# Gate and up of the second feed-forward as seven quarter products (one level of Strassen's algorithm)

## The chip, the cores and the metric

The kernel runs on one core of one Trainium2 chip. The metric is the time of one execution on the device in microseconds (us); lower is better. A core has five engines that run their own instruction queues in order and meet through semaphores: TensorE (PE in the profile; its weight loads have a row of their own, PEld), VectorE (DVE), ScalarE (ACT), GpSimd (POOL) and SyncE (SP), which here issues all DMAs.

## What is computed

Two layers of a transformer over 512 latent and 256 context tokens, model width 1024. Each layer has a token mixer (windowed attention in the first, chunked retention in the second) and a feed-forward, each behind a modulated RMS norm and with a gated residual. After the second layer only the latent tokens are wanted. What the change touches is that layer's feed-forward:

```
def modulate(h, shift, scale):
    return h * (1 + scale) + shift

def swiglu(h, w_in, w_out):
    gate, up = jnp.split(h @ w_in, 2, axis=-1)
    return (jax.nn.silu(gate) * up) @ w_out

x = x + mx[5] * swiglu(modulate(rms_norm(x, norm2_g[i]), mx[3], mx[4]), ffn_w_in[i], ffn_w_out[i])
```

Its hidden width is 2816, which is 22 column tiles of 128. Everything is float32.

## The kernel before, in words

Activations lie transposed: a tile is 128 features (partitions) by tokens, so the 1024 features of the latent stream are eight tiles of 128x512.

**Three matmuls for one.** A float32 product is made of three fast ones. Each operand is split into a rounded part (hi, `fp32r`) and the rest (lo = value - hi). `mm3` (L134) issues hi*hi, lo*hi and hi*lo into the same PSUM tile; `project` (L142) does so for the eight feature tiles, 24 matmuls in a row. Weights go through `next_w` (L120): a DMA brings 128x1024 floats into `wraw` (two buffers), ACT casts them to `whi` (L130), DVE subtracts to get `wlo` (L131). A pair whi/wlo lives in a buffer of the pool `rp` or of the stage's own pool, two of each, in turn. `split` (L146) does the same for activations: ACT casts (L147), DVE subtracts (L148).

**The last head of the retention mixer** ends with `out_tile` (L1019): for each half of the tokens (`HALVES`, 256 each) and each of eight output tiles d, twelve matmuls into a PSUM tile `pv`, then DVE's gated add into the residual `res` (L1027), then ACT's square and DVE's running sum (`add_square`, L191 and L192). After a half is done, `rms` makes the reciprocal root on PE (L199), ACT (L102, L178) and DVE (L179, L180), and `modulate` (L208) makes that half of the feed-forward's operand: DVE multiplies into `hn` (L211), ACT adds the shift and rounds to hi (L214), DVE makes lo (L215). The first half's modulation stands in the middle of the second half's output tiles.

**The feed-forward**, `ffn` (L757), runs over the column tiles in groups of 2, 4, 4, 4, 4 and 4 (`FFN_GROUPS`). `hidden` (L765) makes one tile: `project` with the gate's weights and with the up's weights into the two halves of the PSUM tile `gu` (twice 24 matmuls of 512 columns; the first two tiles go by halves of 256 tokens, so that they can begin when half of the operand is there), then SiLU on ACT (L107), the product with up on DVE (L785), and a split into `ax`. `output` (L791) multiplies a finished group with its rows of the output weights: eight output tiles d, for a group of four 12 matmuls of 512 columns each into `pj` (two PSUM buffers), and DVE's gated add (L225). It stands behind the first hidden tile of the next group. The last one writes the result out by DMA.

**Order.** The code above gives instructions in program order; a scheduler then sets each engine's static order from its own estimate of readiness, and buffers are handed out in that order. On the chip each engine runs its queue strictly as set.

Of the kernel before, what the change touches and what calls it, by code (L numbers as in the profile page):

```python
# [9 lines left out]
F32R = mybir.dt.float32r  # L10
# [4 lines left out]
P = 128  # L15
D = 1024
KT = D // P
SX = 512
SC = 256
# [11 lines left out]
HALVES = (slice(0, 256), slice(256, 512))  # L31
# [21 lines left out]
def dit_kernel(ctx, tc, xT, cT, crow, small, consts, masks, tabs0, tabs1, jtab, adaQ, adaN, adaT, wst, out):  # L53
    nc = tc.nc
    mult, add, sub = ALU.mult, ALU.add, ALU.subtract
# [21 lines left out]
    mods = {(l, s): cp.tile([P, 6, 8], F32, name=f"mod{l}{s}") for l in range(2) for s in range(2)}  # L77
# [28 lines left out]
    def silu(out_, in_):  # L106
        ins = nc.scalar.activation(out_, in_, AF.Silu)  # L107
        after(ins, turn["silu"][:1] or turn["lnexp"])
        turn["silu"].append(ins)
# [7 lines left out]

    wpos, wsel = [0], [0]

    def next_w(pool, own=2):  # L120

        raw = T(rp, 1024, "wraw", 2)
        nc.sync.dma_start(raw, wst[wpos[0]])
        bufs = own
        if wsel[0] % (2 + own) < 2:
            pool, bufs = rp, 2
        wpos[0] += 1
        wsel[0] += 1
        hi, lo = T(pool, 1024, "whi", bufs, F32R), T(pool, 1024, "wlo", bufs, F32R)
        nc.scalar.copy(hi, raw)  # L130
        nc.vector.tensor_tensor(lo, raw, hi, op=sub)  # L131
        return hi, lo
# [9 lines left out]
    def project(w, hs, o):  # L142
        for k in range(KT):
            mm3(o, (w[0][:, k * P:(k + 1) * P], w[1][:, k * P:(k + 1) * P]), hs[k], k == 0, k == KT - 1)

    def split(t, hi, lo):  # L146
        nc.scalar.copy(hi, t)  # L147
        return nc.vector.tensor_tensor(lo, t, hi, op=sub)  # L148


    def load_stream(s):
        res = []
        if s == 0:
            for k in range(KT):
                t = T(rp, 512, "res", 12)
                nc.sync.dma_start(t, xT[:, k, :])
                res.append(t)
        else:
            for k in range(0, KT, 2):
                t = T(rp, 512, "res", 12)  # L160
# [41 lines left out]
    def h_tiles(s):  # L202
        hi = T(rp, 512, "h", 24, F32R)
        if s == 0:
            return hi, T(rp, 512, "h", 24, F32R)
        return hi[:, 0:SC], hi[:, SC:2 * SC]

    def modulate(l, s, which, k, res, h, c=slice(None), tmp=t_hn):  # L208
        y = ssq[s][:, c]
        t = tmp(y.shape[1])  # L210
        nc.vector.scalar_tensor_tensor(t, res[k][:, c], acol[l, s, which][:, k:k + 1], y, mult, mult)  # L211
        hi, lo = h[0][:, c], h[1][:, c]
        b = mods[l, s][:, 3 * which, k:k + 1]
        nc.scalar.activation(hi, t, AF.Identity, bias=b)  # L214
        return nc.vector.scalar_tensor_tensor(lo, t, b, hi, add, sub)  # L215
# [8 lines left out]
    def gated_add(s, l, part, d, o, res):  # L224
        nc.vector.scalar_tensor_tensor(res[d], o, mods[l, s][:, part, d:d + 1], res[d], mult, add)  # L225
# [105 lines left out]
    h = [[], []]  # L331
    raw = []
# [360 lines left out]
    t1 = cp.tile([P, 8], F32, name="lg_t1")  # L693
    t2 = cp.tile([P, 8], F32, name="lg_t2")
# [33 lines left out]
    xr = load_stream(0)  # L728
# [25 lines left out]
    A.close()  # L754


    def ffn(l, streams, hs, halves, extra, done, ahead=()):  # L757


        F = ExitStack()  # L760
        psF = F.enter_context(tc.tile_pool(name="psF", bufs=1, reuse_waits="tile", space=PSUM))
        fp = F.enter_context(tc.tile_pool(name="fp", bufs=1, reuse_waits="tile"))
        count = [0]

        def hidden(act, first):  # L765
            w = ahead.pop(0) if ahead else [next_w(fp), next_w(fp)]
            if count[0] == SHIFT_AT:
                wsel[0] += 2
            for s, _ in streams:
                n = NTOK[s]  # L770
                if s == 0:
                    gu = T(psF, 1024, "gu", 2)
                    hi, lo = T(fp, 512, "ax", 11, F32R), T(fp, 512, "ax", 11, F32R)
                else:
                    gu = T(psF, 512, "guc", 2)
                    hl = T(fp, 512, "ac", 6, F32R)
                    hi, lo = hl[:, 0:SC], hl[:, SC:]
                go, uo = gu[:, 0:n], gu[:, n:2 * n]
# [6 lines left out]
                nc.vector.tensor_tensor(t, t, uo, op=mult)  # L785
                last = split(t, hi, lo)
                act[s].append((hi, lo))
            extra(count[0], first, fp, [last])
            count[0] += 1

        def output(act, gsz, final):  # L791
            nd = 1024 // (gsz * P)
            w = []

            def one(s, res, d):
                while len(w) * nd <= d:
                    w.append(next_w(fp))
                wd = w[d // nd]
                o = pj(NTOK[s])
                for k in range(gsz):  # L800
                    c0 = k * nd * P + (d % nd) * P
                    mm3(o, (wd[0][:, c0:c0 + P], wd[1][:, c0:c0 + P]), act[s][k], k == 0, k == gsz - 1)
                gated_add(s, l, 5, d, o, res)
                if final:
                    done(s, d, res[d])

            if final:
                for s, res in streams:
                    for d in range(KT):
                        one(s, res, d)  # L810
            else:
                for d in range(KT):
                    for s, res in streams:
                        one(s, res, d)

        prev = None
        for gsz in FFN_GROUPS:
            act = {s: [] for s, _ in streams}
            for f in range(gsz):
                hidden(act, f == 0)  # L820
                if f == 0 and prev is not None:
                    output(*prev, False)
            prev = (act, gsz)
        output(*prev, True)
        F.close()
# [27 lines left out]
    hx, _ = norm_mod(0, 0, 1, xr)  # L853
    hc, _ = norm_mod(0, 1, 1, cres)
# [12 lines left out]
    h = [norm_mod(1, 0, 0, xr)[0], norm_mod(1, 1, 0, cres)[0]]  # L867
# [36 lines left out]
    for hd in range(RH):  # L904

        o = []
        for i in range(2):
            w = wq[i] if hd == 0 else next_w(qp)
# [5 lines left out]
        o = []  # L914
# [68 lines left out]
        r, z = mv[:, 8:12], mv[:, 12:16]  # L983
# [19 lines left out]
        for e in range(4):  # L1003
            w = next_w(qp)
            go = pj()
# [23 lines left out]
        if hd < RH - 1:  # L1029
            for d in range(KT):  # L1030
                out_tile(d, slice(0, SX))
            continue
        hx = [h_tiles(0) for _ in range(KT)]
        ln_exp_turn()
        for i, c in enumerate(HALVES):
            for d in range(KT):
                out_tile(d, c)
                add_square(0, d, xr[d], c)
                if i == 1 and d == 1:
                    rms(0, HALVES[0])  # L1040
                    for k in range(KT):
                        modulate(1, 0, 1, k, xr, hx[k], HALVES[0])
        ahead = [[next_w(None), next_w(None)]]
        rms(0, HALVES[1])
        for k in range(KT):
            modulate(1, 0, 1, k, xr, hx[k], HALVES[1])
    R.close()

    ffn(1, ((0, xr),), (hx,), 2, lambda *_: None, lambda s, k, t: nc.sync.dma_start(out[:, k, :], t), ahead)

# [141 lines left out]
```

## Time and profile before

| | |
|---|---|
| median of 3 runs | 1854.78 us (1852.64 to 1856.34) |
| the profiled execution | 1854.34 us |
| its span, first to last instruction | 1852.5 us (1.8 us lie around it) |
| mean granted TensorE clock | 0.993 |
| first and last matmul of the second feed-forward | start at 1485.65 and 1848.41 us of the span |
| first matmul of its third column tile | 1510.78 us |

Times on a row of the trace are microseconds from the start of the span, then the duration of the row. "x2" means two instructions shown as one row. In square brackets stands how long the engine sat idle before, and the engine, tile and line that ended the wait. In the groups by line, the numbers after the bar are the busy time in us and the mean duration of one instruction in ns. A matmul's duration reaches from its issue to its last result, so that neighbours overlap; the time that it takes from the engine is the distance from one start to the next, called the pitch below. The same holds in a small way for DVE and ACT.

### The profile page before, as it was taken

How to read it: one execution, taken by the hardware profiler on the slowest of the kernel's cores; microseconds unless marked ns; L12 is line 12 of the kernel's file. 1: busy time of each engine (PE TensorE's matmuls, PEld its weight loads, DVE VectorE, ACT ScalarE, POOL GpSimd, SP SyncE). 2: the span in 40 equal slices, each digit the busy share in tenths (PEclk: the TensorE clock that was granted, in tenths of full speed). 3: DMA queues.
4: the chain of work that ended last, by engine and by line, in shares of the span. 5: the costliest groups of instructions: out<-in, count | busy, mean ns of one | idle time of the engine just before them, and what ended most of it. 6: DMA issues, size and time to landing. Idle time of an engine off the chain costs nothing.

```text
span 1852.5 us, 24666 instructions
## 1 busy us (share of the span) xinstructions
PE 1798.5 (97%) x9969; PEld 1517.3 (82%) x9969; DVE 1032.3 (56%) x1808; ACT 629.2 (34%) x1064; POOL 150.1 (8%) x243
## 2 busy tenths in 40 slices
PE   5999999899999999999999999999999999999999
PEld 4877776788888888888878888888888888888887
DVE  6787776978555545363684552653543663443343
ACT  5576676351211212121252322422322442222221
POOL 0044443310000000000010010010010000000000
PEclk9999999999999999999999999999999999999999
DMA  9100035525323324261521220320321133333332
GB/s 344 47 24 24 1 108 159 190 93 158 114 92 105 102 91 151 85 205 52 167 82 35 80 80 23 98 85 21 94 69 46 57 99 96 102 92 102 92 102 80
DMA packets 50946, 177.98 MB, mean 96 GB/s; under 512 B 5648, under 2 KB 6032, under 8 KB 50576
## 3 DMA queue, kind: packets, MB, share of 16 engines
q1 hardware_dynamic: 50832, 176.41, 29.9%
q8 instruction: 78, 1.28, 0.3%
q14 instruction: 36, 0.29, 0.1%
HBM read 174.29 MB, written 2.10 MB: 95 GB/s over the span
## 4 chain that ended last, share of the span: by engine, by line
PE 86%; DVE 6%; ACT 3%; DMA 2%; POOL 2%; issue 2%; SPq 0%; DVEq 0%; ACTq 0%; POOLq 0%
PE pj L138 9%; PE pj L139 9%; PE pj L140 9%; PE gu L138 9%; PE gu L139 9%; PE gu L140 9%; PE guc L140 2%; PE guc L139 2%; PE guc L138 2%; PE pT L635 2%; PE pv L138 2%; PE pv L140 2%; PE pv L139 2%; PE pv L943 2%; PE pv L944 2%; PE pv L942 2%
## 5 line engine op out<-in xcount | busy, mean ns | idle before, releaser
L130 ACT CAST whi<-wraw 128x1024 fp32r<-128x1024 f32 x212 | 222.2, 1048 | 387.8 <-PE pj L140 200.5
L131 DVE TENSOR_TENSOR wlo<-wraw,whi 128x1024 fp32r<-128x1024 f32 x212 | 264.7, 1248 | 153.3 <-ACT whi L130 152.5
L138 PE MATMUL gu<-h,whi 128*128 128x512 f32 (+1 forms) x736 | 281.0, 383 | 3.0 <-DVE res L1027 3.0
L139 PE MATMUL gu<-h,wlo 128*128 128x512 f32 (+1 forms) x736 | 280.8, 383 | 0.0
L140 PE MATMUL gu<-h,whi 128*128 128x512 f32 (+1 forms) x736 | 280.4, 382 | 0.0
L138 PE MATMUL pj<-h,whi 128*128 128x512 f32 (+1 forms) x512 | 185.3, 362 | 6.9 <-DVE res L225 6.1
L139 PE MATMUL pj<-h,wlo 128*128 128x512 f32 (+1 forms) x512 | 182.1, 356 | 1.0 <-DVE wlo L131 1.0
L140 PE MATMUL pj<-h,whi 128*128 128x512 f32 (+1 forms) x512 | 181.9, 356 | 0.0
L225 DVE SCALAR_TENSOR_TENSOR res<-pj,mod,res 128x512 f32<-128x512 f32 (+1 forms) x160 | 104.7, 656 | 128.7 <-PE pj L140 128.6
L138 PEld LDWEIGHTS gu<-h,whi 128*128 128x128 f32 x736 | 139.4, 190 | 28.7 <-ACT h L214 3.2
L140 PEld LDWEIGHTS gu<-h,whi 128*128 128x128 f32 x736 | 139.6, 190 | 26.3
L139 PEld LDWEIGHTS gu<-h,wlo 128*128 128x128 f32 x736 | 139.4, 190 | 25.4
L248 DVE CUSTOM_DVE_ANT_0 junk<-adaw,crow_sb,small_sb 128x1024 bf16<-128x1024 f32 x100 | 134.9, 1349 | 36.7 <-DMA adaw<-in_adaT_dram 32.9
L138 PE MATMUL pj<-ax,whi 128*128 128x512 f32 x352 | 138.4, 393 | 0.0
L139 PE MATMUL pj<-ax,wlo 128*128 128x512 f32 x352 | 137.5, 391 | 0.0
L140 PE MATMUL pj<-ax,whi 128*128 128x512 f32 x352 | 137.0, 390 | 0.0
L107 ACT ACTIVATE hn<-gu 128x512 f32<-128x512 f32 x44 | 26.3, 598 | 285.3 <-PE gu L140 285.3
L138 PEld LDWEIGHTS pj<-h,whi 128*128 128x128 f32 x512 | 98.7, 193 | 21.0 <-DVE res L225 7.2
L139 PEld LDWEIGHTS pj<-h,wlo 128*128 128x128 f32 x512 | 98.6, 193 | 13.0 <-DVE wlo L131 1.4
L140 PEld LDWEIGHTS pj<-h,whi 128*128 128x128 f32 x512 | 98.6, 193 | 12.1 <-issue 0.4
L785 DVE TENSOR_TENSOR hn<-hn,gu 128x512 f32<-128x512 f32 x44 | 30.2, 687 | 134.6 <-ACT hn L107 134.6
L140 PE MATMUL guc<-h,whi 128*128 128x256 f32 x352 | 99.8, 284 | 0.0
(249 smaller groups left out, 3417.6 us busy)
## 6 DMA issues: line engine op xcount, KB each, us to landing
wraw<-in_wst_dram SPq DMA_DIRECT2D x214, 512.0 KB, 3.5
adaw<-in_adaT_dram SPq DMA_DIRECT2D x68, 512.0 KB, 4.0
adan<-in_adaQ_dram SPq DMA_DIRECT2D x16, 512.0 KB, 8.1
wraw<-in_adaN_dram SPq DMA_DIRECT2D x12, 512.0 KB, 4.0
res<-in_xT_dram SPq DMA_DIRECT2D x16, 256.0 KB, 4.8
res<-in_cT_dram SPq DMA_DIRECT2D x8, 256.0 KB, 6.8
crow_sb<-in_crow_dram SPq DMA_DIRECT2D x2, 1024.0 KB, 6.0
out_dram<-res SPq DMA_DIRECT2D x8, 256.0 KB, 2.0
```

The costliest lines, as they stand in the source:

```text
L130: nc.scalar.copy(hi, raw)
L131: nc.vector.tensor_tensor(lo, raw, hi, op=sub)
L138: nc.tensor.matmul(o, whi, xhi, start=first, stop=False)
L139: nc.tensor.matmul(o, wlo, xhi, start=False, stop=False)
L140: nc.tensor.matmul(o, whi, xlo, start=False, stop=last)
L225: nc.vector.scalar_tensor_tensor(res[d], o, mods[l, s][:, part, d:d + 1], res[d], mult, add)
L248: after(nc.vector.tensor_tensor_reduce(junk, w, row, 1.0, bias, mult, add, col), behind)
L635: nc.tensor.transpose(tp[:, a * P:(a + 1) * P], self.pr[(0, 2, 1, 3)[a]][:, ki * P:(ki + 1) * P], ident)
L785: nc.vector.tensor_tensor(t, t, uo, op=mult)
L942: nc.tensor.matmul(vo, hi[:, tok], wk_[0][:, cs], start=k == 0, stop=False)
L943: nc.tensor.matmul(vo, hi[:, tok], wk_[1][:, cs], start=False, stop=False)
L944: nc.tensor.matmul(vo, lo[:, tok], wk_[0][:, cs], start=False, stop=k == KT - 1)
```

## The change

The operand A (tokens by features) is cut in two along tokens and in two along features: A11 is tokens 0 to 255 with features 0 to 511, A12 has the other features, A21 and A22 the other tokens. The weights B of one column tile are cut along features and into gate and up: B11 and B21 are the gate's feature halves, B12 and B22 the up's. From the third column tile on, gate and up (four blocks of 256 tokens by 128 columns) come from seven products of quarters instead of eight:

```
S1 = A21+A22  S2 = S1-A11  S3 = A11-A21  S4 = A12-S2
T1 = B12-B11  T3 = B22-B12  T2 = B22-T1  -T4 = B21-T2
P1 = A11*B11  P2 = A12*B21  P3 = S4*B22  P4' = A22*(-T4)  P5 = S1*T1  P6 = S2*T2  P7 = S3*T3
gate, tokens 0-255   = P1+P2              up, tokens 0-255   = P1+P6 + P5+P3
gate, tokens 256-511 = P1+P6+P7+P4'       up, tokens 256-511 = P1+P6+P7 + P5
```

- `modulate` gets an optional target: for this norm the product before the shift is kept in eight more tiles `hm` (tag `h`) instead of the two rotating `hn` buffers.
- `sums`, called ahead of the second column tile, makes S1 to S4 from `hm` and the shifts in place, 16 DVE instructions of 256 columns, and splits them into 16 tiles `sA`: eight casts on ACT and eight subtractions on DVE, 512 columns each.
- `hidden_seven` makes a column tile from the third on. Per tile: two DMAs as before; three pairs whi/wlo and one half pair (B22, in two tiles of tag `h`) instead of two pairs; four DVE subtractions of 512 columns for the T's; seven products of four feature tiles by three matmuls of 256 columns (84 matmuls instead of 48 of 512 columns) in the PSUM tiles X, Y, Z; four ACT copies out of PSUM; three DVE additions of 256 columns; SiLU in two halves; the product with up and its split as before. Y is accumulated on after each copy: P1, then P6, then P7, then P4'; so the product that follows a copy by one has to wait until the copy has read.
- The pool of the second feed-forward has four pairs whi/wlo of its own instead of two, and two raw buffers of its own.
- The first feed-forward, the first two column tiles of the second and the outputs keep their arithmetic.

```diff
-    def next_w(pool, own=2):
-        raw = T(rp, 1024, "wraw", 2)
+    def w_raw(pool=None, bufs=2):
+        raw = T(pool or rp, 1024, "wraw", bufs)
         nc.sync.dma_start(raw, wst[wpos[0]])
...
-    def modulate(l, s, which, k, res, h, c=slice(None), tmp=t_hn):
+    def modulate(l, s, which, k, res, h, c=slice(None), t=None):
         y = ssq[s][:, c]
-        t = tmp(y.shape[1])
+        if t is None:
+            t = t_hn(y.shape[1])
...
+        own = 4 if hm else 2
+        def sums():
+            q1, q2 = HALVES
+            shift = mods[l, 0][:, 3]
+            sh2 = T(fp, 8, "sh2", 1)
+            nc.vector.tensor_tensor(sh2[:, 0:4], shift[:, 0:4], shift[:, 4:8], op=add)
+            for k in range(4):
+                t1, t2 = hm[k], hm[k + 4]
+                nc.vector.scalar_tensor_tensor(t2[:, q2], t1[:, q2], sh2[:, k:k + 1], t2[:, q2], add, add)
+                nc.vector.tensor_tensor(t1[:, q2], t1[:, q1], t1[:, q2], op=sub)
+                nc.vector.scalar_tensor_tensor(t1[:, q1], t2[:, q2], shift[:, k:k + 1], t1[:, q1], sub, sub)
+                nc.vector.scalar_tensor_tensor(t2[:, q1], t2[:, q1], shift[:, k + 4:k + 5], t1[:, q1], add, sub)
+                for t in (t2, t1):
+                    sA.append((T(fp, 512, "sA", 16, F32R), T(fp, 512, "sA", 16, F32R)))
+                    split(t, *sA[-1])
+        def hidden_seven(act):
+            g, u = w_raw(fp, 2), w_raw()
...
+            split(g, *b["11"])
+            nc.vector.tensor_tensor(g[:, l_], u[:, l_], g[:, l_], op=sub)
+            split(u[:, r_], *b["22"])
+            nc.vector.tensor_tensor(u[:, l_], u[:, r_], u[:, l_], op=sub)
+            nc.vector.tensor_tensor(u[:, r_], u[:, r_], g[:, l_], op=sub)
+            nc.vector.tensor_tensor(g[:, r_], g[:, r_], u[:, r_], op=sub)
+            split(u, *b["32"])
+            split(g, *b["14"])
...
+            product(Y, "11", "11", 0, True)
+            nc.scalar.copy(p1, Y)
+            product(Z, 1, "14", 0, True)
+            nc.scalar.copy(z1, Z)
+            product(Y, 2, "32", 512, False)
+            nc.scalar.copy(u2, Y)
+            product(X, "12", "11", 512, True)
+            nc.vector.tensor_tensor(t[:, HALVES[0]], p1, X, op=add)
+            silu(t[:, HALVES[0]], t[:, HALVES[0]])
+            product(Y, 3, "32", 0, False)
+            nc.scalar.copy(u3, Y)
+            product(Z, 4, "22", 0, False)
+            nc.vector.tensor_tensor(up[:, HALVES[0]], u2, Z, op=add)
+            product(Y, "22", "14", 512, False)
+            nc.vector.tensor_tensor(up[:, HALVES[1]], u3, z1, op=add)
+            silu(t[:, HALVES[1]], Y)
+            nc.vector.tensor_tensor(t, t, up, op=mult)
...
         def hidden(act, first):
-            w = ahead.pop(0) if ahead else [next_w(fp), next_w(fp)]
+            if hm and count[0] >= 2:
+                return hidden_seven(act)
+            if hm and count[0] == 1:
+                sums()
+            w = ahead.pop(0) if ahead else [next_w(fp, own), next_w(fp, own)]
...
+        hm = [T(rp, 512, "h", 24) for _ in range(KT)]
```

More of the change, by code (lines that the diff above doesn't have):

```diff
@@ L118, in dit_kernel, with w_parts @@
     wpos, wsel = [0], [0]
-    def next_w(pool, own=2):
-        raw = T(rp, 1024, "wraw", 2)
+    def w_raw(pool=None, bufs=2):
+        raw = T(pool or rp, 1024, "wraw", bufs)
         nc.sync.dma_start(raw, wst[wpos[0]])
+        wpos[0] += 1
+        return raw
+    def w_parts(pool, own=2):
         bufs = own
@@ L126, in next_w @@
             pool, bufs = rp, 2
-        wpos[0] += 1
         wsel[0] += 1
-        hi, lo = T(pool, 1024, "whi", bufs, F32R), T(pool, 1024, "wlo", bufs, F32R)
+        return T(pool, 1024, "whi", bufs, F32R), T(pool, 1024, "wlo", bufs, F32R)
+    def next_w(pool, own=2):
+        raw = w_raw()
+        hi, lo = w_parts(pool, own)
         nc.scalar.copy(hi, raw)
@@ L754, in dit_kernel, with ffn @@
     A.close()
-    def ffn(l, streams, hs, halves, extra, done, ahead=()):
+    def ffn(l, streams, hs, halves, extra, done, ahead=(), hm=None):
         F = ExitStack()
@@ L763, in ffn @@
         count = [0]
-        def hidden(act, first):
-            w = ahead.pop(0) if ahead else [next_w(fp), next_w(fp)]
+        own = 4 if hm else 2
+        sA = []
+        def sums():
[12 more added lines that the diff above has]
+                    split(t, *sA[-1])
@@ new lines, in operand_a, with product @@
+        def operand_a(n):
+            if isinstance(n, int):
+                return lambda k: [a[:, HALVES[n % 2 if n < 3 else n == 3]] for a in sA[2 * k + (n in (2, 3))]]
+            c, k0 = HALVES[n[0] == "2"], 4 * (n[1] == "2")
+            return lambda k: [a[:, c] for a in hs[0][k0 + k]]
+        def hidden_seven(act):
+            g, u = w_raw(fp, 2), w_raw()
+            b = {"11": w_parts(fp, own)}
+            b["22"] = T(rp, 512, "h", 24, F32R), T(rp, 512, "h", 24, F32R)
+            b["14"], b["32"] = w_parts(fp, own), w_parts(fp, own)
+            l_, r_ = slice(0, 512), slice(512, 1024)
+            split(g, *b["11"])
[6 more added lines that the diff above has]
+            split(g, *b["14"])
+            def product(o, a, n, c0, first):
+                x = operand_a(a)
+                for k in range(4):
+                    ws = slice(c0 + k * P, c0 + (k + 1) * P)
+                    (whi, wlo), (xhi, xlo) = (a[:, ws] for a in b[n]), x(k)
+                    for i, (p, r) in enumerate(((whi, xhi), (wlo, xhi), (whi, xlo))):
+                        nc.tensor.matmul(o, p, r, start=first and k + i == 0, stop=k == 3 and i == 2,
+                                         skip_group_check=not first)
+            X, Y, Z = (T(psF, 512, n, 2)[:, 0:SC] for n in "XYZ")
+            t, up = t_hn(SX), t_sq(SX)
+            e1, e2 = T(rp, 512, "res", 12), T(rp, 512, "res", 12)
+            p1, z1, u2, u3 = e1[:, HALVES[0]], e1[:, HALVES[1]], e2[:, HALVES[0]], e2[:, HALVES[1]]
+            product(Y, "11", "11", 0, True)
[15 more added lines that the diff above has]
+            nc.vector.tensor_tensor(t, t, up, op=mult)
+            hi, lo = T(fp, 512, "ax", 11, F32R), T(fp, 512, "ax", 11, F32R)
+            split(t, hi, lo)
+            act[0].append((hi, lo))
+            count[0] += 1
@@ L771, in hidden @@
                 if s == 0:
-                    gu = T(psF, 1024, "gu", 2)
+                    gu = None if hm else T(psF, 1024, "gu", 2)
                     hi, lo = T(fp, 512, "ax", 11, F32R), T(fp, 512, "ax", 11, F32R)
@@ L777, in hidden @@
                     hi, lo = hl[:, 0:SC], hl[:, SC:]
-                go, uo = gu[:, 0:n], gu[:, n:2 * n]
+                go, uo = (gu[:, 0:n], gu[:, n:2 * n]) if gu else (T(psF, 512, "X", 2), T(psF, 512, "Y", 2))
                 for c in HALVES if count[0] < halves else (slice(0, n),):
@@ L796, in one @@
                 while len(w) * nd <= d:
-                    w.append(next_w(fp))
+                    w.append(next_w(fp, own))
                 wd = w[d // nd]
@@ L1041, in dit_kernel @@
                     for k in range(KT):
-                        modulate(1, 0, 1, k, xr, hx[k], HALVES[0])
+                        modulate(1, 0, 1, k, xr, hx[k], HALVES[0], hm[k][:, HALVES[0]])
         ahead = [[next_w(None), next_w(None)]]
@@ L1045, in dit_kernel @@
         for k in range(KT):
-            modulate(1, 0, 1, k, xr, hx[k], HALVES[1])
+            modulate(1, 0, 1, k, xr, hx[k], HALVES[1], hm[k][:, HALVES[1]])
     R.close()
-    ffn(1, ((0, xr),), (hx,), 2, lambda *_: None, lambda s, k, t: nc.sync.dma_start(out[:, k, :], t), ahead)
+    ffn(1, ((0, xr),), (hx,), 2, lambda *_: None, lambda s, k, t: nc.sync.dma_start(out[:, k, :], t), ahead, hm)
 def _cols(w, n0, n):
```

## Prediction

> **What bounds the kernel now.** The first view is the page's summary: busy time of each engine and the shares of the chain that ended last.
>
> ```profile
> span 1852.5 us, 24666 instructions
> ...
> PE 1798.5 (97%) x9969; PEld 1517.3 (82%) x9969; DVE 1032.3 (56%) x1808; ACT 629.2 (34%) x1064; POOL 150.1 (8%) x243
> ...
> PE 86%; DVE 6%; ACT 3%; DMA 2%; POOL 2%; issue 2%; SPq 0%; DVEq 0%; ACTq 0%; POOLq 0%
> ```
>
> TensorE is the bound: busy for 97% of the span and 86% of the chain. Whether this holds where the change acts, the windows say: the third to the last column tile with all outputs, and one whole group (four hidden tiles and an output).
>
> ```profile
> core 0: us, PE busy (x) PEld busy (x) DVE busy (x) ACT busy (x) POOL busy (x), PEclk, DMA share, GB/s
> ...
> 1510.78:1848.60 337.82, 337.82 (x1490) 279.12 (x1488) 134.05 (x148) 83.12 (x101) 0.00 (x0) 1.00 0.31 96
> 1554.83:1620.11 65.28, 65.28 (x289) 54.10 (x288) 26.01 (x29) 16.75 (x20) 0.00 (x0) 1.00 0.35 108
> ```
>
> PE never rests there, at full clock; VectorE is busy for 40% and ScalarE for 25%. A group holds 288 matmuls of 512 columns: pitch 65.28/288 = 0.2267 us, 10.88 us for a hidden tile's 48. So a microsecond less on PE is one less in all, as long as the other two deliver.
>
> **The matmuls.** The pitch at 256 columns is read from the second column tile, which already runs so (start times in the timeline of PE, first and last of 64 steps):
>
> ```profile
> 1503.10 0.28 PE L139 MATMUL gu<-h,wlo 128*128 128x256 f32 x1
> ...
> 1510.78 0.40 PE L138 MATMUL gu<-h,whi 128*128 128x512 f32 x1
> ```
>
> 7.68/64 = 0.120 us, more than half of 0.2267: some 7 ns per matmul do not shrink with the columns. A tile of seven products takes 84 x 0.120 = 10.08 us instead of 10.88. **Twenty tiles: -16.0 us**; the columns fall by an eighth (84 x 256 for 48 x 512), the time of a tile by 7%.
>
> The Trainium skill, "TensorE: Matmul & The Clock Gate", section "Back-to-back issue gap", gives a warm gap of N/2.4 + 2.5 ns, 109 and 216 ns here. By it a tile would save 1.19 us and the change 23.7 before its costs. The rows say 120 and 227 ns on this very kind of instruction, and the measurement decides.
>
> **What a tile costs the other engines.** Groups by line, then two starts that give a pitch:
>
> ```profile
> L131 DVE TENSOR_TENSOR wlo<-wraw,whi 128x1024 fp32r<-128x1024 f32 x66 | 80.8, 1225 | 85.8 <-ACT whi L130 85.8
> ...
> L785 DVE TENSOR_TENSOR hn<-hn,gu 128x512 f32<-128x512 f32 x22 | 15.1, 688 | 74.2 <-ACT hn L107 74.2
> L148 DVE TENSOR_TENSOR ax<-hn,ax 128x512 fp32r<-128x512 f32 x22 | 15.1, 685 | 0.0
> L215 DVE SCALAR_TENSOR_TENSOR h<-hn,mod,h 128x256 fp32r<-128x256 f32 x16 | 7.3, 479 | 0.5 <-ACT h L214 0.5
> ```
> ```profile
> 1546.66 0.69 DVE L148 TENSOR_TENSOR ax<-hn,ax 128x512 fp32r<-128x512 f32 x1
> 1547.27 1.22 DVE L131 TENSOR_TENSOR wlo<-wraw,whi 128x1024 fp32r<-128x1024 f32 x1
> ```
> ```profile
> L130 ACT CAST whi<-wraw 128x1024 fp32r<-128x1024 f32 x66 | 69.2, 1048 | 154.2 <-issue 69.0 <-PE pj L140 52.5 <-PE gu L140 26.9
> L147 ACT CAST ax<-hn 128x512 fp32r<-128x512 f32 x22 | 13.6, 620 | 0.0
> ```
> ```profile
> L107 ACT ACTIVATE sq<-guc 128x256 f32<-128x256 f32 x22 | 8.5, 384 | 38.9 <-PE guc L140 38.9
> ```
>
> Back to back, DVE's 512 columns take 0.61 us and its 1024 columns 1.14 (below). A new tile asks of DVE three low parts of 1024 columns (3.4), six instructions of 512 for low parts and T's, two more for the product and its split (8 x 0.61 to 0.69, say 5.2) and three additions of 256 (1.0): 9.6 us where it was 3.7; of ACT three casts of 1.05, two of 0.62, four copies and two SiLUs of 256 columns (0.38 to 0.42, the nearest row is the SiLU out of `guc`): 6.8 us. Both stay below PE's 10.08, DVE narrowly; in the 21.8 us of an output it has only ten to do, and the built order puts the preparation of the next two tiles there. So in the mean it is hidden.
>
> The wait to fear is a new one. Y is written on after each copy, with one product (1.44 us) between, and ACT runs in order. In the built order the copy of a tile's first product stands behind the preparation of the tile after next (cast of its first weights, DVE's T chain, cast of a T) and behind the split of the tile before. The loop, from the end of a tile's X product (it frees the buffer for those weights): cast 1.05, low part 1.14, then DVE in order add 0.33, T1 0.61, add 0.34, T3 0.69, T2 0.69; cast 0.95, split 0.49, copy 0.40; with handoffs 6.9 us. Behind the copy wait the P6 and P2 products, 2.88 and 0.17 of drain: 9.9 us around, against 10.08. **Margin 0.2 us**, in two tiles of each group of four, the others having their weights from the output. I take 0.1 us for some eight tiles, **+0.9 us** with the first group; bounds 0 and 0.6 us for each of eighteen.
>
> **The start** costs most. At the end of the mixer PE waits for DVE's gated adds (timeline of PE; the last rows show the clock after that idle):
>
> ```profile
> 1478.63 0.39 PE L138 MATMUL pv<-yt,whi 128*128 128x256 f32 x1 [0.21 <-DVE res L1027]
> ...
> 1480.95 0.39 PE L138 MATMUL pv<-yt,whi 128*128 128x256 f32 x1 [0.64 <-DVE res L1027]
> ...
> 1485.65 0.55 PE L138 MATMUL gu<-h,whi 128*128 128x256 f32 x1 [3.03 <-DVE res L1027]
> 1486.00 0.42 PE L139 MATMUL gu<-h,wlo 128*128 128x256 f32 x1
> ...
> 1488.99 0.30 PE L138 MATMUL gu<-h,whi 128*128 128x256 f32 x1
> ```
> ```profile
> 1477.37 0.42 DVE L192 TENSOR_TENSOR y<-y,sq 128x256 f32<-128x256 f32 x1
> 1477.70 0.48 DVE L215 SCALAR_TENSOR_TENSOR h<-hn,mod,h 128x256 fp32r<-128x256 f32 x1
> 1478.10 0.48 DVE L1027 SCALAR_TENSOR_TENSOR res<-pv,mod,res 128x256 f32<-128x256 f32 x1
> 1478.49 0.48 DVE L215 SCALAR_TENSOR_TENSOR h<-hn,mod,h 128x256 fp32r<-128x256 f32 x1
> 1478.89 0.88 DVE L211 SCALAR_TENSOR_TENSOR hn<-res,acol,y 128x256 f32<-128x256 f32 x2
> ...
> 1480.41 0.48 DVE L1027 SCALAR_TENSOR_TENSOR res<-pv,mod,res 128x256 f32<-128x256 f32 x1
> ...
> 1485.04 0.47 DVE L1027 SCALAR_TENSOR_TENSOR res<-pv,mod,res 128x256 f32<-128x256 f32 x1
> ...
> 1485.82 1.21 DVE L131 TENSOR_TENSOR wlo<-wraw,whi 128x1024 fp32r<-128x1024 f32 x1
> 1486.96 0.41 DVE L192 TENSOR_TENSOR y<-y,sq 128x256 f32<-128x256 f32 x1
> ...
> 1491.17 0.42 DVE L179 SCALAR_TENSOR_TENSOR sq<-pj,sq 128x256 f32<-128x256 f32 x1 [2.66 <-ACT sq L178]
> ...
> 1499.59 0.89 DVE L215 SCALAR_TENSOR_TENSOR h<-hn,mod,h 128x256 fp32r<-128x256 f32 x2 [0.18 <-ACT h L214]
> ```
>
> Pitches on DVE: 256 columns 0.33 (two operands) and 0.40 (with a scalar), 1024 columns 1.14. Between two gated adds stand four modulation instructions, 2.31 us; with eight `hm` tiles instead of two `hn`, the built order has two, 1.53 us. The fifth add comes near 1477.4, so the eighth near 1482.0 instead of 1485.04. Behind it follow 25 modulation instructions (10.0), a sum (0.3), two low parts (2.3), the root (0.9) and waits for ACT, one of them for a cast that follows a DMA of 3.5 us:
>
> ```profile
> wraw<-in_wst_dram SPq DMA_DIRECT2D x214, 512.0 KB, 3.5
> ```
>
> I allow 1.5 for these: the operand is complete at 1497.4 instead of 1500.48 (bounds 1496.5 and 1500.5).
>
> Now the sums. In the built order PE does, behind the first tile, two products of the third tile (24 matmuls) and then tile two, whose second matmul needs a low part that stands on DVE behind 19 instructions: ten with a scalar (4.0, in place, not in this trace; 4.8 at full duration), four differences (1.3), the first tile's product (0.7), five low parts of 512 (3.05), then itself (1.23): 10.3 us. So tile two resumes at 1507.7, where PE has waited for some 3.3 us. The row at 1485.65 shows what that does: 14 matmuls in 2.99 us from 1486.00, 0.214 each, 1.3 us lost. 94 matmuls are left: 94 x 0.120 + 1.3 = 12.6, end 1520.3; the rest of the sums and the third tile's weights are ready by then (9 us of DVE behind that low part). Of the third tile 2.88 us are done. The old kernel stood there at 1510.78: **+6.6 us** (1520.3 - 2.88 - 1510.78).
>
> The Trainium skill, same page, section "Part 1: The HAM clock gate", has the clock halve after an idle window of about 3.4 us that runs freely; the row agrees, after 3.03 us. A wait of 3.3 may miss such a window; the sum would then be 1.3 us less.
>
> At the end the last output waits for SiLU, product and split of the last tile as before, with 256 columns of SiLU instead of 512 (0.38 for 0.60): nothing.
>
> **Sum**, against the profiled execution (1854.34: span 1852.5 and 1.84 around it; 0.4 below the median, no matter here): 1854.3 - 16.0 + 6.6 + 0.9 = **1845.8 us**.
>
> **The rivals.**
> - *The start is dearer.* The operand is no earlier (3.1 us more) and the third tile's T's, whose raw weights are fetched only when tile two's low part frees their buffer, come late by some 2 us: 1849 to 1851. For it: the root of the second half follows a cast that waits for a DMA, and DVE has 46 instructions to do there before and after alike; against it: the rows at 1478 to 1485 show PE and DVE waiting on each other, which the new order loosens.
> - *VectorE's and ScalarE's chain becomes the bound* (the slower side). If the loop of 9.9 us takes over 10.08, PE stops before P6 or P7 of each tile in a row of four. It decides from 10.76 us on for each of eighteen tiles (18 x 0.68 = 12.2 us: then 0.2% slower); with 0.15 us more at each of eight handoffs the loop is 11.1 and 18 x 1.02 are lost: 1863. For it: DVE at 9.6 of 10.08 and a margin of 0.2; against it: two tiles are prepared ahead during each output, and only two of four tiles have the whole chain.
> - *Short matmuls are quicker*, the page's gap, or the sums hide: 1838. Against it the 0.120 of the row.
> - *No saving at all*: 84 matmuls with their 84 weight loads at 0.1295 instead of 0.120 would make a tile equal: 1861. The row excludes nearly that.
>
> **How the numbers follow.** Forecast 0.62 (own range 1841 to 1850.5), dear start 0.18, bound chain 0.13, quicker 0.05, no saving 0.02. The range 1840 to 1857 leaves out the last two and most of the bound chain, under 2 in 10. About 0.2%, 3.7 us, is what a measurement of this kernel can tell from none: faster means below 1851.1, slower above 1858.5. Faster: 0.62 + 0.05 + a part of the dear start, 0.72; slower: most of the bound chain and the last, 0.13; within: 0.15.
>
> **What would show it.** Steps of 0.120 in the seven products and 10.08 us a tile; groups 62.1 us apart instead of 65.28; one PE wait of about 3 us for DVE's low part ahead of tile two's second matmul, with slow matmuls behind it; first matmul of the stage near 1482.5; PE waits on ACT's copies below 0.2 us. Wrong if PE waits on copies in every tile, if DVE has no idle time within four hidden tiles, or if the T's of the third tile stop PE.

## The result, and the profile after

The changed kernel takes **1847.4 us** (median of 7 runs, 1841.2 to 1850.7) against 1853.7 (7 runs, 1851.2 to 1856.3): ratio 0.996, 95% interval 0.9947 to 0.9974. That is faster, by 6.3 us in the medians. The profiled execution of after took 1843.17 us at a granted clock of 0.995; the other six lie between 0.990 and 0.997, and the shorter times go with the higher clock.

The page of after, summary and chain shares:

```profile
span 1841.4 us, 26454 instructions
...
PE 1782.3 (97%) x10689; PEld 1532.7 (83%) x10689; DVE 1147.5 (62%) x2013; ACT 694.0 (38%) x1212; POOL 150.1 (8%) x243
...
PE 83%; DVE 7%; ACT 3%; DMA 3%; issue 2%; POOL 2%; SPq 0%; ACTq 0%; DVEq 0%; POOLq 0%
```

TensorE remains the bound, with 16 us less work. PE's waits from 1470 us to the end (engine, tile and line, what it waited for, then us in total, times, longest):

```profile
PE X L147 <- DVE wlo L139: 2.9, 1, 2.9
PE Y L146 <- ACT whi L138: 1.4, 1, 1.4
PE X L146 <- DVE res L1118: 1.3, 1, 1.3
PE X L146 <- ACT whi L138: 1.1, 1, 1.1
PE X L146 <- ACT h L223: 0.9, 2, 0.4
PE Z L823 <- ACT res L833: 0.8, 1, 0.8
PE Y L823 <- ACT res L835: 0.2, 1, 0.2
```

The 3.0 us for the gated add have become 1.3. The new 2.9 us is tile two's low part, behind the sums. All copies together cost 1.0, but none of it is for the copy of a tile's first product (L831). The 0.8 is at the third tile, where the next copy stood on ACT behind a cast of the output's weights that had waited 2.4 us for its DMA (timeline of ACT):

```profile
1518.70 1.05 ACT L138 CAST whi<-wraw 128x1024 fp32r<-128x1024 f32 x1 [2.40 <-DMA wraw<-in_wst_dram]
...
1520.17 0.36 ACT L833 COPY res<-Z 128x256 f32<-128x256 f32 x1
```

**A ruler for two traces.** The profiles differ by some microseconds ahead of the change, so spans are a poor measure. The matmul that sums the first half's squares is the last mark that stands in both programs after the same instructions; over the twelve profiles it starts between 1470.0 and 1475.2 us. From it to the start of the last matmul, before and then after (timelines of PE):

```profile
1472.03 0.59 PE L199 MATMUL pj<-y,ones_sb 128*128 128x256 f32 x2
...
1848.41 0.39 PE L140 MATMUL pj<-ax,whi 128*128 128x512 f32 x1
```
```profile
1470.89 0.59 PE L207 MATMUL pj<-y,ones_sb 128*128 128x256 f32 x2
...
1481.39 0.36 PE L146 MATMUL X<-h,whi 128*128 128x256 f32 x1 [1.26 <-DVE res L1118]
...
1505.14 0.38 PE L147 MATMUL X<-h,wlo 128*128 128x256 f32 x1 [2.88 <-DVE wlo L139]
...
1516.54 0.28 PE L823 MATMUL Z<-sA,whi 128*128 128x256 f32 x1
...
1837.26 0.40 PE L148 MATMUL pj<-ax,whi 128*128 128x512 f32 x1
```

376.38 us before, 366.37 after: **10.0 us less**; a further 1.1 of the profiled difference stands ahead of the change. The interval on the runs allows 4.8 to 9.8. Tile two ends at 1516.54 with 2.88 us of the third tile done, so the third tile stands at 1513.66, 42.8 us after the mark; before it was 38.75. The start therefore loses 4.0 us, and from there to the end 14.0 are won (323.6 for 337.6).

DVE at the start of after:

```profile
1476.21 0.48 DVE L1118 SCALAR_TENSOR_TENSOR res<-pv,mod,res 128x256 f32<-128x256 f32 x1
1477.73 0.48 DVE L1118 SCALAR_TENSOR_TENSOR res<-pv,mod,res 128x256 f32<-128x256 f32 x1
...
1493.78 1.27 DVE L224 SCALAR_TENSOR_TENSOR h<-h,mod 128x256 fp32r<-128x256 f32 x3
1494.97 0.87 DVE L787 SCALAR_TENSOR_TENSOR h<-h,sh 128x256 f32<-128x256 f32 x2
...
1503.88 1.22 DVE L139 TENSOR_TENSOR wlo<-wraw,whi 128x1024 fp32r<-128x1024 f32 x1
```

Gated adds 1.52 apart as forecast; the operand is complete at 1495.0; between it and the end of tile two's low part DVE works 10.1 us without a gap, mostly at the sums (forecast 10.3). PE waits 1.1 and 1.4 us for tile two's `whi` as well, ahead of that low part; what ends last is the low part.

A group of after (window from one gate's first half to that of the group behind):

```profile
1562.34:1624.54 62.20, 62.20 (x434) 57.84 (x433) 46.68 (x64) 28.58 (x48) 0.00 (x0) 1.00 0.35 102
```

62.2 us instead of 65.28, forecast 62.1. But its inside is not as forecast. From X product to X product (timeline of PE), three hidden tiles and then one with an output:

```profile
1727.08 0.28 PE L823 MATMUL X<-h,whi 128*128 128x256 f32 x1
...
1737.00 0.28 PE L823 MATMUL X<-h,whi 128*128 128x256 f32 x1
...
1746.98 0.28 PE L823 MATMUL X<-h,whi 128*128 128x256 f32 x1
...
1756.91 0.28 PE L823 MATMUL X<-h,whi 128*128 128x256 f32 x1
...
1789.15 0.28 PE L823 MATMUL X<-h,whi 128*128 128x256 f32 x1
```

A tile takes 9.92 to 9.98, less than 84 x 0.120 = 10.08, and an output 22.3 instead of 96 x 0.2267 = 21.76. The outputs' arithmetic was untouched, yet most of their matmuls have a pitch of 0.2333, while most of the short ones of the products have 0.118. The trace holds no addresses; they follow from the order and the sizes of the tiles in a pool. In the built program the small tile `sh2` (8 columns, 32 bytes a partition) pushes `sA` and the stage's own weight pairs 32 bytes off; `ax`, `h` and the older weight pairs stay where they were. In after, 0.2333 falls to 0.2267 just where an output's weights lie in the older pairs.

### The profile page after: what moved, and what is told of

Read it like the earlier page. It is cut to its first block, busy times and chain, and to the rows that moved or that the text cites. A ratio compares the mean times of both kernels' runs of the same rounds, so it can differ in the third digit from the quotient of the medians.

```text
span 1841.4 us, 26454 instructions
## 1 busy us (share of the span) xinstructions
PE 1782.3 (97%) x10689; PEld 1532.7 (83%) x10689; DVE 1147.5 (62%) x2013; ACT 694.0 (38%) x1212; POOL 150.1 (8%) x243
## 4 chain that ended last, share of the span: by engine, by line
PE 83%; DVE 7%; ACT 3%; DMA 3%; issue 2%; POOL 2%; SPq 0%; ACTq 0%; DVEq 0%; POOLq 0%
PE pj L146 9%; PE pj L147 9%; PE pj L148 9%; PE Y L823 6%; PE gu L146 4%; PE gu L147 4%; PE gu L148 4%; PE Z L823 3%; PE guc L148 2%; PE guc L147 2%; PE guc L146 2%; PE pv L146 2%; PE pv L148 2%; PE pv L147 2%; PE pT L644 2%; PE pv L1034 2%
## 5 line engine op out<-in xcount | busy, mean ns | idle before, releaser
L138 ACT CAST whi<-wraw 128x1024 fp32r<-128x1024 f32 x172 | 180.2, 1048 | 248.6 <-PE pj L148 147.2
L139 DVE TENSOR_TENSOR wlo<-wraw,whi 128x1024 fp32r<-128x1024 f32 x172 | 215.6, 1254 | 82.2 <-ACT whi L138 80.9
L146 PE MATMUL gu<-h,whi 128*128 128x512 f32 x352 | 137.6, 391 | 0.0
L147 PE MATMUL gu<-h,wlo 128*128 128x512 f32 x352 | 137.1, 390 | 0.0
L148 PE MATMUL gu<-h,whi 128*128 128x512 f32 x352 | 137.0, 390 | 0.0
L148 PE MATMUL guc<-h,whi 128*128 128x256 f32 x352 | 99.6, 283 | 0.0
L147 PE MATMUL guc<-h,wlo 128*128 128x256 f32 x352 | 99.6, 283 | 0.0
L146 PE MATMUL guc<-h,whi 128*128 128x256 f32 x352 | 99.5, 283 | 0.0
L155 ACT CAST whi<-wraw 128x1024 fp32r<-128x1024 f32 x62 | 64.3, 1050 | 66.8 <-PE pj L148 28.8
L107 ACT ACTIVATE hn<-gu 128x512 f32<-128x512 f32 x22 | 13.2, 598 | 198.6 <-PE gu L148 198.6
L156 DVE TENSOR_TENSOR res<-pv,res 128x512 fp32r<-128x512 f32 x24 | 16.6, 692 | 112.8 <-ACT res L155 112.8
```

Of the source, the lines that this page charges most:

```text
L146: nc.tensor.matmul(o, whi, xhi, start=first, stop=False)
L147: nc.tensor.matmul(o, wlo, xhi, start=False, stop=False)
L148: nc.tensor.matmul(o, whi, xlo, start=False, stop=last)
```

## The experiments

Two questions: whether the gain and its losses come from where the prediction put them (products, sums ahead of the low part, copies' loop), and what the pitches depend on. Rivals: the gain comes from the earlier operand; the pitch is set by what precedes the matmuls. The stage's four weight pairs and its own raw buffers were not tried alone. "Stage" is the time from the mark to the last matmul; the ratio is to the kernel before, on the same chip.

| run | median us | ratio (95%) | stage us |
|---|---|---|---|
| before | 1853.7 to 1854.4 | | 376.4 |
| after | 1847.4 | 0.9960 (0.9947 to 0.9974) | 366.4 |
| e1_hm_only | 1851.4 | 0.9986 (0.9978 to 0.9995) | 374.6 |
| e2_sh2_64 | 1844.7 | 0.9951 (0.9934 to 0.9967) | 366.5 |
| e3_shift_before | 1859.6 | 1.0029 (1.0020 to 1.0038) | 381.0 |
| e4_w_first | 1842.8 | 0.9937 (0.9922 to 0.9952) | 363.3 |
| e5_from12 | 1855.0 | 1.0005 (0.9996 to 1.0014) | 377.1 |
| e6_copy3 | 1852.9 | 0.9994 (0.9985 to 1.0003) | 373.8 |
| e7_sh2_128 | 1846.6 | 0.9965 (0.9953 to 0.9977) | 368.1 |
| e8_aligned | 1846.2 | 0.9959 (0.9947 to 0.9972) | 366.2 |
| e9_first_offset | **1839.0** | 0.9919 (0.9906 to 0.9932) | 361.4 |
| e10_no_sums | 1841.8 | 0.9936 (0.9923 to 0.9949) | 362.7 |

**e1_hm_only: the earlier operand alone.** In after the feed-forward is called without `hm`:

```diff
-    ffn(1, ((0, xr),), (hx,), 2, ..., ahead, hm)
+    ffn(1, ((0, xr),), (hx,), 2, ..., ahead)
```

> The kernel before with one piece of the change: the modulation keeps its products in the eight tiles hm (they are not used for anything else), the two rotating buffers are free. No sums, no seven products, two weight pairs as before. Theory (the order of the mixer's end carries much of the gain): the eighth gated add comes 3 us earlier and the operand is complete some 4 us earlier, as in the profile of after (1.52 us between gated adds instead of 2.31; last modulation at 1495.0 instead of 1500.5, of which 1.1 us is a difference that stands ahead of the change), PE has nothing else to wait for: 1849.5 to 1850.7 against 1853.7. Rival (the products carry the gain, the earlier operand is absorbed by waits for weights): 1853.7.

Stage 1.8 us shorter, medians 3.1 (interval 0.9 to 4.1), where 3.0 to 4.2 were expected: a gain, in the trace smaller than expected. PE's waits at the start:

```profile
PE gu L146 <- DVE res L1118: 1.3, 1, 1.3
PE gu L146 <- ACT h L223: 0.6, 2, 0.4
PE pj L207 <- DVE y L200: 0.3, 1, 0.3
PE gu L147 <- DVE wlo L139: 0.2, 1, 0.2
```

The wait for the gated add falls from 3.0 to 1.3, but several small ones follow, and the third tile stands only 1.8 us earlier (36.9 after the mark for 38.75). So of after's 10.0 us the mixer's order gives 1.8, the rest of the new start takes 5.9 (42.8 for 36.9; e4 and e10 below say how much of it is the sums), and 14.0 come from the third tile on.

**e3_shift_before: 32 bytes in the old kernel.**

```diff
+            if l == 1 and count[0] == 1:
+                nc.gpsimd.memset(T(fp, 8, "pad", 1), 0.0)
```

> The kernel before with nothing but a tile of 32 bytes a partition put into the second feed-forward's pool behind ax, so that half of the weight pairs begin 32 bytes off. Theory (addresses): 720 of its 1488 matmuls of 512 columns from 0.2267 to 0.2333, +4.8 us, 96 of 256 columns 0.2 us less: 1858.3 against 1853.7. Rival (phase, or the change's own instructions): 1853.7, pitch 0.2267 throughout.

+4.7 us in the stage, +5.2 in the medians (interval 3.7 to 7.0): as the address theory said. One output of it, of which the first four tiles d use weights 32 bytes off and the last four the older pairs:

```profile
1574.78 0.39 PE L138 MATMUL pj<-ax,whi 128*128 128x512 f32 x1
...
1585.97 0.39 PE L138 MATMUL pj<-ax,whi 128*128 128x512 f32 x1
...
1596.87 0.39 PE L138 MATMUL gu<-h,whi 128*128 128x512 f32 x1
```

48 matmuls in 11.19 us (0.233), then 48 in 10.90 (0.227). The whole stage alternates so, by weight pair.

**e2_sh2_64 and e7_sh2_128: 64 and 128 bytes.**

```diff
-            sh2 = T(fp, 8, "sh2", 1)
+            sh2 = T(fp, 16, "sh2", 1)      # e7: 32 columns
```

> The changed kernel with the small tile sh2 of 64 bytes a partition instead of 32, so that all tiles of the second feed-forward's pool begin at multiples of 64 bytes. In after the weight pairs of that pool and sA begin 32 bytes off, ax, h and the other weight pairs do not. Theory (matmuls of 512 columns whose two operands lie differently against 64 bytes take 0.2333 us instead of 0.2267, those of 256 columns 0.1183 instead of 0.1200): outputs all at 0.2267 (384 matmuls at 0.0067 less, -2.6 us), products all at 0.1200 (1008 at 0.0017 more, +1.7): 1846.5 against 1847.4, within the spread of the times but plain in the pitches of the trace. Rival (the pitch is set by the phase of loads and matmuls after the short products): outputs stay at 0.2333 for most.

> As e2, with sh2 of 128 bytes a partition: the pool's weight pairs and sA begin 128 bytes off. Known from the traces: at 32 and 64 bytes off matmuls of 512 columns take 0.233 us instead of 0.2267, those of 256 columns 0.118 and 0.116 instead of 0.120. Theory A (what counts repeats every 128 bytes): as with no offset, outputs 0.2267, products 0.1200, no gain against after (-0.5). Theory B (it repeats at 512 bytes or more): outputs stay at 0.233, the short products become quicker still, 0.114 or less where the operands lie apart: 3 to 4 us less than after from the root's matmul to the last.

e2 contradicts the theory as stated there, and not its core: 64 bytes off is also off, the outputs stay at 0.2333. Short products came out at 0.116 in the mean where the operands lie apart, and mostly at 0.120 where they lie alike. In e7 the outputs with shifted weights take 0.2321 to 0.2328 (24 matmuls in 5.57 to 5.59 us), those with the older pairs 0.227 to 0.228; short products whose operands lie apart take 0.119. So theory A fails: the effect does not repeat at 128 bytes. Theory B was right that the outputs stay near 0.233 and wrong about the products, which become no quicker.

**e8_aligned: no offset.**

```diff
-            sh2 = T(fp, 8, "sh2", 1)
+            sh2 = acol[0, 0, 0]
```

> The changed kernel with sh2 in a spent tile of layer 0 and no tile of its own: every operand lies alike against 512 bytes. Theory (what counts is the distance of the two operands' addresses): all 528 output matmuls at 0.2267 (2.6 us less than after), all 1680 of the products at 0.1200 (2.1 more): a column tile 10.08 us and a run from output to output 62.1 as predicted, 1846.5 to 1847 in all. Rival (the 0.233 belongs to what precedes the outputs): 0.233 stays.

The X products of the same group as shown for after:

```profile
1727.20 0.28 PE L823 MATMUL X<-h,whi 128*128 128x256 f32 x1
...
1737.28 0.28 PE L823 MATMUL X<-h,whi 128*128 128x256 f32 x1
...
1747.36 0.28 PE L823 MATMUL X<-h,whi 128*128 128x256 f32 x1
...
1757.44 0.28 PE L823 MATMUL X<-h,whi 128*128 128x256 f32 x1
...
1789.30 0.28 PE L823 MATMUL X<-h,whi 128*128 128x256 f32 x1
```

10.08 each and 31.86 = 10.08 + 21.78 with an output: to the hundredth what the prediction had. From the third tile to the end 322.1 us instead of 337.6: 15.5 won, where the prediction had 16.0 - 0.9. In total e8 equals after: it is 1.5 us shorter from the third tile on, and loses 1.3 more at the start, by a half clock that after's profile does not have (below).

**e5_from12: the slope.** `count[0] >= 12` instead of 2, with e8's layout.

> Seven products only from the thirteenth column tile on (10 tiles instead of 20); tiles three to twelve by whole products of 512 columns into X and Y. The sums stay where they are, and sh2 lies in a spent tile of 32 bytes of layer 0, so that all weight pairs, sA, ax and h lie alike against 512 bytes. Compare it with e8, which has the same layout. Theory (0.8 us a tile on PE: 48 x 0.2267 against 84 x 0.1200): 8.0 us more than e8 from the root's matmul to the last one, so about 374 us there against 376.4 in before; some 1853. Rival (the products are dearer than their matmuls, or the T's and copies cost PE time): less than 6 us between the two.

Stage 377.1, 10.9 more than e8 instead of 8.0. 2.1 of these lie ahead of the third tile, where the waits for wlo and whi were 4.1 and 2.8 us in this order instead of 2.9 and 1.3 and the half clock lasted 10.2 us instead of 3.4; behind it 8.8 for ten tiles, 0.7 of it one wait for a gated add: 0.8 us a tile. With half of the tiles the kernel is no faster than before: what ten tiles win pays for the dearer start.

**e6_copy3: 0.75 us more in the copies' loop.** `nc.scalar.copy(p1, Y)` stands three times.

> The changed kernel with the copy of each tile's first product made three times on ACT instead of once: 0.75 us more in the loop from the end of the X product over the preparation to that copy and back. Theory (the loop of 9.8 to 9.9 us stands next to PE's 10.0, margin 0.1 to 0.2): about 0.6 us lost in each tile whose weights are prepared within the run of four, 9 to 18 of 20, so 5 to 11 us more than after: 1853 to 1858, with a PE wait for this copy in each. Rival (preparation runs ahead over the four weight pairs and takes up the delay): 1847 to 1848, no new waits.

1852.9 and 7.4 us more in the stage: 1.5 of them at the start (a half clock behind the wait, below), 5.9 from the third tile on. Groups, by the second gated add of two outputs in succession (after, then e6):

```profile
1579.62 0.74 DVE L234 SCALAR_TENSOR_TENSOR res<-pj,mod,res 128x512 f32<-128x512 f32 x1
...
1641.79 0.75 DVE L234 SCALAR_TENSOR_TENSOR res<-pj,mod,res 128x512 f32<-128x512 f32 x1
```
```profile
1582.98 0.74 DVE L234 SCALAR_TENSOR_TENSOR res<-pj,mod,res 128x512 f32<-128x512 f32 x1
...
1646.60 0.74 DVE L234 SCALAR_TENSOR_TENSOR res<-pj,mod,res 128x512 f32<-128x512 f32 x1
```

62.2 becomes 63.6. The lower end of what the loop said and not the rival's nothing: the margin is small. The edit changed more than the copies, though: the scheduler reacted to them and moved other products between, which hid a part. The waits that the trace names are fewer than expected (1.6 us in four). The rest is in smaller pieces at the same place: the starts around the first matmul of a Y product with `sA`, which follows a copy, are further apart than 0.120 by 8.2 us in all, against 0.9 in after.

**e4_w_first: tile two's weights ahead of the sums.**

```diff
-            if hm and count[0] == 1:
-                sums()
             w = ahead.pop(0) if ahead else [next_w(fp, own), next_w(fp, own)]
+            if hm and count[0] == 1:
+                sums()
```

> The changed kernel with tile two's two weight pairs asked for ahead of the sums instead of behind them; in the built order DVE then makes tile two's first low part ahead of all sA splits. Theory (tile two waits only because its low part is queued behind the sums on DVE): the PE wait of 2.9 us for wlo goes or falls below 0.5, and since the sums have 11 us of tile two to be finished in, nothing takes its place: 1844.5 to 1845 against 1847.4. Rival (DVE is the bound of the start as a whole): PE waits as long for an sA or a T of the third tile instead, 1847.4.

```profile
PE X L146 <- DVE res L1118: 1.3, 1, 1.3
PE X L146 <- ACT whi L138: 1.1, 1, 1.1
PE X L146 <- ACT h L223: 0.9, 2, 0.4
PE X L147 <- DVE wlo L139: 0.7, 1, 0.7
PE Y L823 <- DVE wlo L156: 0.6, 1, 0.6
PE Z L823 <- ACT whi L155: 0.5, 1, 0.5
```

The wait falls from 2.9 to 0.7, not below 0.5, and the one for whi (1.4) goes; 1.1 come back at the third tile, where nothing was expected. The stage is 3.1 us shorter than after's, the median 4.6. Order, not DVE's amount of work, was what cost most of it.

**e10_no_sums: the sums left out.** `sA` is filled from `hs[0]`, the sums' instructions are gone, and the output is not the layer's.

> The changed kernel without the sums: the 16 instructions that make S1 to S4 and their splits are left out, and the products that use them read tiles of the operand h instead, so the output is not the reference's. The matmuls are as many and as long. Theory (the sums cost some 6 us at the start, because tile two's low part and the third tile's weights stand behind them on DVE): the wait of 2.9 us for wlo and most of the 1.4 for whi go, 5 to 6 us less than after from the root's matmul to the last: 360.5 to 361.5; 1841 to 1842.5. Rival (the start is bound by PE's and DVE's work on tiles one and two without the sums): 2 us less at most, 1845.

Stage 3.7 us shorter than after's, less than the 5 to 6 expected. Both waits went, but a new one came:

```profile
1516.46 0.62 ACT L155 CAST h<-wraw 128x512 fp32r<-128x512 f32 x1 [1.65 <-DMA wraw<-in_wst_dram]
1516.98 0.36 ACT L829 COPY res<-Y 128x256 f32<-128x256 f32 x1
1517.40 0.39 PE L817 MATMUL Y<-h,whi 128*128 128x256 f32 x1 [1.58 <-ACT res L829]
```

The third tile's last copy but one (L829) now stands on ACT behind a cast of coming weights, and that cast waits for its DMA. So of the 5.9 us by which after's start is dearer than e1's, leaving the sums out wins 3.7; 1.6 are lost again to weights that arrive late. e4 gets 3.1 of these 3.7 by order alone.

**e9_first_offset: e4 with a chosen layout.**

```diff
+        if hm:
+            for tag in ("whi", "wlo"):
+                nc.gpsimd.memset(T(fp, 1024, tag, own, F32R)[:, 0:8].bitcast(F32), 0.0)
...
-            sh2 = T(fp, 8, "sh2", 1)
+            sh2 = T(fp, 16, "sh2", 1)
```

> e4 (tile two's weights ahead of the sums) with the pool laid out so that all weight pairs, ax and h lie alike against 512 bytes and only sA lies 64 bytes off. Theory (addresses, as the traces of e2, e7 and e8 gave them: 512 columns 0.2267 alike and 0.233 at 64 bytes off, 256 columns 0.1200 alike and 0.1161 at 64 off): all 528 output matmuls at 0.2267 (288 of them 0.0067 less than in e4, -1.9), 960 of the 1680 product matmuls at 0.1161, 720 at 0.1200 (197.9 us instead of 199.5, -1.6), some of which the copies' loop may hold back: 360 to 361.5 us from the root's matmul to the last one against 363.3 in e4 and 366.4 in after; 1839 to 1841 in all, the quickest so far. Rival (the pitches belong to what happened to precede them): 363, no change against e4.

**1839.0 us**, the best of all, 0.81% below the kernel before (0.68 to 0.94%); stage 361.4. Outputs 0.227 throughout. The product part of the expectation missed: the products with `sA` took 1.42 us for twelve (0.118, not 0.1161), a tile 9.98. So the size of the gain for short matmuls does not follow from the distance to `sA` alone: the product with B22 (a `Z<-sA,h` row of twelve) takes 1.36 us in e2 (from 1732.29 us) and 1.41 in e9 (from 1729.59), both with `sA` 64 bytes off. What else it depends on stays open.

## Why the prediction was right, step by step

It said 1845.8 (1840 to 1857); the median is 1847.4. From its base that is 8.5 us less; the medians differ by 6.3, the profiled stages by 10.0. In after's stage the sum reads -17.6 for the products, +2.6 for the outputs, +4.0 for the start and +1.0 for the copies. The prediction had -16.0, nothing, +6.6 and +0.9.

- **-16.0 from the products.** Right in the aligned layout: 10.08 a tile to the hundredth (e8), 0.8 us a tile by the slope (e5). In after itself the term is about -17.6 (tiles of 10.00 in the mean, without the two waits for copies), by short matmuls of 0.118. One aside is wrong: by pitches of 0.120 and 0.2267 the part of a matmul that does not shrink is 2 x 0.120 - 0.2267, 13 ns, and not 7; the sum does not use it.
- **The outputs keep their time.** A step that the prediction did not even write down, and wrong: 384 of their 528 matmuls went to 0.2333, 2.6 us. Pools were looked at for their order and not for addresses. That it hardly showed in the total is luck: the short matmuls won back 1.6 by the same addresses.
- **+6.6 at the start.** The mechanism was right: gated adds 1.52 apart, the low part 10.1 us behind the operand, a wait of 2.9 us at tile two's second matmul, down to 0.7 when the order is changed (e4). The two waits for tile two's `whi` were not foreseen; they come before the low part is ready and so add nothing to the sum. The size in the profile of after is 4.0. Of the 2.6 difference about 1.3 is the half clock that did not come, and about 1.4 an operand and low part that were earlier (1495.0 and 1505.1, by the mark 1.1 more, against 1497.4 and 1507.7). The term was mis-sized by these two.
- **The half clock behind that wait.** It came in the profiles of e2, e6, e7 and e8, which have the same wait, and of e5, where it began within the wait of 2.8 us ahead of the one of 4.1. The window from the resuming matmul, in e2 and in after:

```profile
1506.85:1512.85 6.00, 6.00 (x28) 6.00 (x29) 6.00 (x10) 1.76 (x3) 0.00 (x0) 0.51 0.61 171
```
```profile
1505.14:1511.14 6.00, 6.00 (x50) 6.00 (x50) 6.00 (x10) 1.77 (x3) 0.00 (x0) 1.00 0.60 165
```

28 matmuls instead of 50, after waits of 2.91 and 2.88. In e2 the clock fell 2.0 us into the wait, at 1505.9, and in e6 0.35 us behind its end. It stayed at half for 3.41 us in e6 and e8, as in the kernel before, for 6.83 in e2 and e7 and for 10.24 in e5: once, twice and three times 3.41. With it the start lost 5.3 (e8) to 6.7 us (e7), which is near the forecast 6.6 by other sizes: the low part was 1.4 earlier, and the half clock cost 1.3 to 2.6 us against after. It may be a part of after's spread, and of why its median lies above its profile; that its longer runs had it is not shown, since they have only a mean clock. The Trainium skill, "TensorE: Matmul & The Clock Gate", section "Part 1: The HAM clock gate", says that the window runs freely; the rows agree: waits alike within 0.05 us did and did not bring it. The idle window of about 3.4 us that the same section gives is longer than these waits of 2.9 us, and than the 3.03 us of the kernel before that the prediction took as agreeing; here the measured waits decide.
- **+0.9 for the chain.** The size is luck. The waits of after sum to 1.0, but not as 0.1 in some eight tiles for the first product's copy: 0.8 of it is one copy behind a cast that waited for its weights' DMA, and no wait is for the first product's copy. That the loop has little margin is right, since 0.75 us more in it costs 5.9 (e6); the 0.2 itself is not measured.
- **Dear start.** Its reasons (operand no earlier, T's late) did not occur in after, where PE waits for no T; e1 shows the earlier operand at work, though of the 3.1 us by which the first matmul comes earlier only 1.8 arrive at the third tile.
- **Quicker short matmuls.** Half true: 0.118 instead of 0.120, from addresses. The Trainium skill, same page, section "Back-to-back issue gap", gives N/2.4 + 2.5 ns for an isolated matmul, 109 ns at 256 columns. No run reached it: the quickest twelve have a pitch of 0.113 us (e2).
- **Slips.** A bound chain at 10.76 us would give 1857.1, which is 0.15% above the kernel before and still below the 1858.5 that the prediction calls slower. The instructions that it lists ahead of tile two's low part are 20, as in the trace, and not 19. Neither touches the sum.

## What to carry to other kernels

A product saved by Strassen's scheme saves columns, not instructions: here 12.5% fewer columns were 7% of a tile, and the dearer start (5.9 us) ate as much as seven of twenty tiles won. What the first tiles need belongs ahead of the sums in the queue of the engine that makes both. When a change adds even a 32-byte tile, compare the pitches of matmuls that it does not touch, and look where their operands came to lie.

## What the hardware showed unexpectedly

- The pitch of an fp32r matmul depends on where moving and stationary operand lie against each other: of 512 columns 0.2267 us alike (modulo 512 bytes), 0.2333 at 32 or 64 bytes apart, 0.2321 to 0.2328 at 128; of 256 columns 0.120 alike, 0.113 to 0.119 apart. Both operands 32 bytes off count as alike (0.120 for `sA` with the shifted weights in after). One 32-byte tile made the old kernel 5 us slower (e3). The mechanism is open.
- PE waits of 2.86 to 2.91 us halved the granted clock in four profiles (e2, e6, e7, e8) and not in a fifth (after). It stayed at half for 3.41 us or for twice that.
